# A fused layer kernel: the final shift laid into the output ahead, scaled rows added to it by accumulating transfers, and short low parts of the last group on GpSimd

## Chip, cores and metric

One core of a Trainium2 chip. The metric is the device time of one execution in microseconds (us); the kernel before was run three times, and one further execution was profiled.

## What is computed

One layer over 2048 positions of width 1024: a normalisation, a projection, convolutions and a gated delta rule, an output projection, a gated feed-forward block (1024 to 2 x 2816, then 2816 to 1024), and a last normalisation with its own scale and shift. Only the end matters here:

```python
        h = adaln(x, g_norm_ffn[layer], shift_f, scale_f)
        gt, up = jnp.split(h @ w_gate_up[layer], 2, axis=-1)
        x = x + gate_f[:, None, :] * ((jax.nn.silu(gt) * up) @ w_down[layer])
    shift_o, scale_o = jnp.split(c_act @ w_ada_final + b_ada_final, 2, axis=-1)
    return adaln(x, g_norm_final, shift_o, scale_o)
```

`adaln(x, g, shift, scale)` divides each row by its root mean square, multiplies by `g` and `1 + scale`, and adds `shift`, which is one row of 1024 numbers that is the same for all positions.

## The kernel before

All matrix products are made from split operands: a value is the sum of a rounded high part (`...h`, made by ScalarE) and a low part (`...l`, the difference, made by VectorE or GpSimd), and a product is three matmuls: high x high, high x low, low x high.

The last stage multiplies the hidden activations by `w_down`. The 2816 features are 22 blocks of 128, taken in pairs, and the pairs in six groups: group 0 has one pair, groups 1 to 5 two each. The outer loop runs over the groups, the inner one over eight slices `s`; a slice stands for two tiles of 128 positions, `(s, 0)` and `(s, 1)`. One (group, slice) is an item. Each tile has an accumulator `acc` (128 x 1024) in SBUF that lives through all groups.

In groups 1 to 5 an item's 2 x 2 block product is made with seven products in place of eight (Strassen's way): A11, S1, A12, S2, S4, S3 and A22, each of two pairs x three matmuls of 512 columns, so 42 matmuls per item. After each product, or second product into the same bank, VectorE adds the PSUM bank to half an accumulator (`add`, L1681, seven per item). S3 and A22 (`p7`, `p4`, the list `late`) are held back and run among the products of the next item. The order within an item is A11, S1, the last item's S3, A12, S2, S4, the last item's A22.

The item after next is loaded by `load_item` (L1542, two pieces `ra` of 448 KB, three buffers, on SyncE's queue). `split_item` (L1554 to 1573) splits the next item's pieces: `xh`, `xl` (5 of the 7 operands, 128 x 640) and `yh`, `yl` (the operands S3 and A22, 128 x 256). The high parts are ScalarE's (L1564). The low parts are subtractions at L1573, on the engine that `lo_engine` names: in groups 1 to 4 the first pair's are VectorE's and the second's GpSimd's; in the last group all are VectorE's.

The weights of the next group are prepared inside a group by `prep_group`: rows of `w_down` are loaded on SyncE's queue (L373), multiplied by a gate on GpSimd (L1610), then combined and split on VectorE and ScalarE. The last group has no such work.

In the last group a tile is finished as soon as its last addition is made, by `finish` (L1687), a generator that is advanced after every six matmuls: ScalarE squares and sums the row (L511), GpSimd makes the inverse root (L505, L506), VectorE scales the accumulator by it and by `go_d`, the gain (L1691), GpSimd adds the shift `so_d` (L1692), and SyncE's queue stores 512 KB (L1694). This is done for 15 tiles; the sixteenth, `(7, 1)`, goes through `finish_last` (L1697 to 1716), which splits the row in parts over the engines (GpSimd L1703, VectorE L1704, L1707, L1708, GpSimd's power L1709, then three pieces and two stores). The rows `go_d` and `so_d` lie in a DRAM row each (`final_d`) and are copied to all partitions once, in group 4 (L1663).

In this stage the order of instructions on an engine is that of a scheduler, not the order of the source: instructions of neighbouring steps may change places.

Of the kernel before, what the change touches and what calls it, by code (L numbers as in the profile page):

```python
# [15 lines left out]
ALU = mybir.AluOpType  # L16
# [4 lines left out]
P = 128  # L21
D = 1024
# [8 lines left out]
CH = BLK // P  # L31
# [169 lines left out]
def layer_kernel(ctx, tc, x, c, w_ada, b_ada, w_ada_final, b_ada_final, g_norm_mix, g_norm_ffn, g_norm_final,  # L201
                 w_in, conv_w_mix, conv_w_qkv, a_log, dt_bias, g_conv_out, g_dn_out, w_out, w_gate_up,
                 w_down, cst, out):
    nc = tc.nc
    x, out = x[0], out[0]
# [15 lines left out]
    def dense_ps():  # L221
        return pd.tile([P, 512], F32, name="pd")

    def misc_ps():
        return pm.tile([P, 512], F32, name="pm")
# [34 lines left out]
    def spawn(gen, delay=1):  # L260
        side.append([gen, delay, gen.__name__ not in FIRST_CHAINS])
        side.sort(key=lambda e: e[2])
# [245 lines left out]
    def sum_squares(t):  # L508
        ss = g0.tile([P, 1], F32, name="ss", bufs=4)
        junk = sp.tile([P, D], mybir.dt.bfloat16, name="ht", bufs=2)  # L510
        nc.scalar.activation(junk, t, AF.Square, accum_out=ss)  # L511
        rms_scale(ss, 1, D)
        return ss
# [149 lines left out]
    with ExitStack() as actx:  # L663
# [119 lines left out]
        for b in range(NB):  # L783
# [434 lines left out]
            for m in range(4):  # L1218
# [9 lines left out]
                u = ap_.tile([P, BLK + 3], F32, name="cb", bufs=2)  # L1228
# [17 lines left out]
            for n in range(2):  # L1246
# [27 lines left out]
                for t in range(CH):  # L1274
                    row = b * CH + t
# [12 lines left out]
    final_d = {n: dr.tile([1, D], F32, name=n) for n in ("go_d", "so_d")}  # L1288
# [89 lines left out]
    def work():  # L1378
        for q in (jobs, sums):
            while q:  # L1380
                try:
                    next(q[0])
                    break
                except StopIteration:
                    q.popleft()

    def work_off():
        while jobs or sums:
            work()
# [140 lines left out]
    last = len(groups) - 1  # L1530
# [3 lines left out]
    def load_item(n):  # L1534
        if n >= len(items):
            return
        g, s = items[n]
        raws[n] = []
        for i in groups[g]:
            w = 4 if i == 0 else 7  # L1540
            raw = dp.tile([P, 7, P], F32, name="ra", bufs=3)[:, :w, :]
            nc.sync.dma_start(raw, actd[s // CH, i][s % CH][:, :w, :])  # L1542
            raws[n].append(raw)
        if g == 0:
            for u in range(2):
                t = dp.tile([P, D], F32, name=f"acc{s}_{u}")
                nc.sync.dma_start(t, x1d[s // CH * 8 + u * CH + s % CH])
                accs[s, u] = t

    def lo_engine(g, q):  # L1550
        return nc.vector if q == 0 and g or g == last else nc.gpsimd


    def split_item(n):  # L1554
        if n >= len(items):
            return
        g, s = items[n]
        acts_d[n], todo = [], []
        for q, (i, raw) in enumerate(zip(groups[g], raws.pop(n))):
            X = {}  # L1560
            for e, c0, c1 in (("x", 0, 5 if i else 4),) + ((("y", 5, 7),) if i else ()):
                hl = [dp.tile([P, 5 if e == "x" else 2, P], F32R, name=e + p, bufs=4 if e == "x" else 6) for p in "hl"]
                hi, lo = (t[:, :c1 - c0, :] for t in hl)
                nc.scalar.copy(hi, raw[:, c0:c1, :])  # L1564
                todo.append((e, lo_engine(g, q), lo, raw[:, c0:c1, :], hi))
                for j in range(c0, c1):
                    X[(ORDER if i else FIRST)[j]] = [t[:, j - c0, :] for t in hl]
            acts_d[n].append(X)
        for e in "xy":
            yield  # L1570
            for f, eng, lo, raw, hi in todo:
                if f == e:
                    eng.tensor_sub(lo, raw, hi.bitcast(F32))  # L1573

    load_item(0)
    ahead = split_item(0)
    next(ahead)
    next(ahead, None)
# [70 lines left out]
    def prep_group(g):  # L1649
        if g <= last:  # L1650
            i, j = groups[g]
            DW[i], DW[j] = {}, {}
            yield from gate_pair(i)
            yield from down_weights(i, lambda: load_pair(j))
            yield
            yield from gate_pair(j)
            yield from down_weights(j, lambda: load_pair(groups[g + 1][0]) if g < last else None)
        if g == last:
            yield
            for n in ("go_d", "so_d", "g"):  # L1660
                fin[n] = wr.tile([P, D], F32, name="wraw")
                src = g_norm_final.rearrange("(o n) -> o n", o=1) if n == "g" else final_d[n]
                nc.sync.dma_start(fin[n], src.to_broadcast([P, D]))  # L1663
            yield
            yield
            yield
            nc.vector.scalar_tensor_tensor(fin["go_d"], fin["go_d"], 1.0, fin["g"], op0=ALU.add, op1=ALU.mult)

    fin = {}

    def dproduct(ps, parts, start):
        for q, (a, w) in enumerate(parts):
            (ah, al), (wh, wl) = a, w
            first = dict(start=start and q == 0, skip_group_check=not start)
            dmm(ps, ah, wh, stop=False, **first)
            first["start"] = False
            dmm(ps, ah, wl, stop=False, **first)
            dmm(ps, al, wh, stop=q == len(parts) - 1, **first)

    def add(s, u, ns, ps):  # L1680
        nc.vector.tensor_add(accs[s, u][:, ns], accs[s, u][:, ns], ps)  # L1681

    def row(s, u):
        r = s // CH * 8 + u * CH + s % CH
        return slice(r * P, (r + 1) * P)

    def finish(s, u):  # L1687
        t = accs[s, u]
        ss = sum_squares(t)
        yield 3  # L1690
        nc.vector.scalar_tensor_tensor(t, t, ss, fin["go_d"], op0=ALU.mult, op1=ALU.mult)  # L1691
        nc.gpsimd.tensor_add(t, t, fin["so_d"])  # L1692
        yield 2
        nc.sync.dma_start(out[row(s, u), :], t)  # L1694


    def finish_last(s, u):  # L1697
# [22 lines left out]
    for n, (g, s) in enumerate(items):  # L1720
        if s == 0:
            work_off()
            jobs.append(prep_group(g + 1))
        G, X = groups[g], acts_d.pop(n)
        ahead = split_item(n + 1)

        def parts(a, w):
            return [(x[a], DW[i][w]) for x, i in zip(X, G)]

        if g == 0:  # L1730
            for q in range(4):
                p = dense_ps()
                u, c0 = q // 2, q % 2
                r, cl = "A" + "12"[u], "12"[c0]
                dproduct(p, [(X[0][r + k], DW[0]["B" + k + cl]) for k in "12"], True)
                add(s, u, (h0, h1)[c0], p)
                if q == 0:
                    next(ahead, None)
                    load_item(n + 2)
                elif q == 1:  # L1740
                    for _ in ahead:
                        pass
                work()
            continue
        a, b, c_ = dense_ps(), misc_ps(), misc_ps()
        dproduct(a, parts("A11", "B11"), True)
        add(s, 0, h0, a)
        next(ahead, None)
        dproduct(c_, parts("S1", "T1"), True)
        add(s, 1, h1, c_)  # L1750
        work()
        if late:
            late[0]()
        next(ahead, None)
        dproduct(b, parts("A12", "B21"), True)
        add(s, 0, h0, b)
        work()
        dproduct(a, parts("S2", "T2"), False)
        add(s, 0, h1, a)
        next(ahead, None)  # L1760
        load_item(n + 2)
        dproduct(c_, parts("S4", "B22"), False)
        add(s, 0, h1, c_)
        work()
        if g == last:
            spawn(finish(s, 0), 1)
        if late:
            late[1]()
        work()

        def p7(a=a, s=s, q=parts("S3", "T3")):
            dproduct(a, q, False)
            add(s, 1, h1, a)

        def p4(a=a, s=s, q=parts("A22", "T4"), g=g):
            dproduct(a, q, False)
            add(s, 1, h0, a)
            if g == last and s < 2 * CH - 1:
                spawn(finish(s, 1), 1)

        late = p7, p4
# [27 lines left out]
```

## Time and profile before

| | |
|---|---|
| median of 3 runs | 2486.65 us (2485.29 to 2488.56) |
| the profiled execution, its own time | 2487.72 us |
| its span in the profile | 2485.9 us |
| busy, whole span: TensorE | 2356.5 us (95%) |
| VectorE | 1833.5 us (74%) |
| ScalarE | 1024.0 us (41%) |
| GpSimd | 644.7 us (26%) |
| mean rate of the transfers | 136 GB/s |

PE is TensorE, PEld its weight loads, DVE VectorE, ACT ScalarE, POOL GpSimd, SP SyncE (a q behind it: its queue). L1681 is line 1681 of the kernel. Times in the timeline are us from the start of the span. A busy share is an average over the whole program; a stretch of its own has its own limit, and the last group, some 90 us, is 4% of the span. The ends of matmuls are modelled and overlap: one lasts 0.39 us in the rows while they follow each other every 0.23 us.

### The profile page before, as it was taken

How to read it: one execution, taken by the hardware profiler on the slowest of the kernel's cores; microseconds unless marked ns; L12 is line 12 of the kernel's file. 1: busy time of each engine (PE TensorE's matmuls, PEld its weight loads, DVE VectorE, ACT ScalarE, POOL GpSimd, SP SyncE). 2: the span in 40 equal slices, each digit the busy share in tenths (PEclk: the TensorE clock that was granted, in tenths of full speed). 3: DMA queues.
4: the chain of work that ended last, by engine and by line, in shares of the span. 5: the costliest groups of instructions: out<-in, count | busy, mean ns of one | idle time of the engine just before them, and what ended most of it. 6: DMA issues, size and time to landing. Idle time of an engine off the chain costs nothing. (4 is left out here: it accounts for less than half of the span.)

```text
span 2485.9 us, 30764 instructions
## 1 busy us (share of the span) xinstructions
PE 2356.5 (95%) x11243; PEld 1937.9 (78%) x11243; DVE 1833.5 (74%) x2610; ACT 1024.0 (41%) x1771; POOL 644.7 (26%) x688
## 2 busy tenths in 40 slices
PE   5889999999899999998999999999999999999996
PEld 4778877888778877886878888878888877887774
DVE  6897759875897659788566566875665668888898
ACT  3633555344643464355543333533333323332232
POOL 2632255032722255212000000000000045444336
PEclk9999999999999999999999999999999999999999
DMA  7442446524452344236673333753433373333433
GB/s 244 119 106 68 145 140 174 156 90 155 138 149 78 118 148 111 69 115 199 193 234 108 92 115 101 245 169 94 119 101 99 106 269 131 119 120 106 137 126 115
DMA packets 397534, 336.98 MB, mean 136 GB/s; under 512 B 39475, under 2 KB 338748, under 8 KB 397382
## 3 DMA queue, kind: packets, MB, share of 16 engines
q1 hardware_dynamic: 397126, 334.91, 44.0%
q8 instruction: 88, 1.44, 0.2%
q14 instruction: 64, 0.52, 0.1%
q10 hardware_dynamic: 256, 0.10, 0.0%
HBM read 261.55 MB, written 73.41 MB: 135 GB/s over the span
## 5 line engine op out<-in xcount | busy, mean ns | idle before, releaser
L378 ACT CAST whi<-wraw 128x1024 fp32r<-128x1024 f32 x278 | 291.8, 1050 | 389.2 <-PE pd L311 191.4
L380 DVE TENSOR_TENSOR wlo<-wraw,whi 128x1024 fp32r<-128x1024 f32 x275 | 346.4, 1260 | 98.0 <-ACT whi L378 91.3
L311 PE MATMUL pd<-hTh,whi 128*128 128x512 f32 x896 | 369.7, 413 | 1.8 <-DVE hTh L540 1.6
L311 PE MATMUL pd<-hTl,whi 128*128 128x512 f32 x896 | 354.3, 395 | 1.8 <-DVE hTl L541 1.8
L311 PE MATMUL pd<-hTh,wlo 128*128 128x512 f32 x896 | 354.6, 396 | 1.5 <-DVE wlo L380 1.5
L1487 POOL TENSOR_TENSOR wraw<-wraw 128x1024 f32<-128x1024 f32 x2 | 5.0, 2504 | 780.3 <-DMA wraw<-in_w_down_dram 780.3
L311 PEld LDWEIGHTS pd<-hTh,wlo 128*128 128x128 f32 x896 | 170.7, 191 | 39.6 <-DVE wlo L380 2.4
L311 PEld LDWEIGHTS pd<-hTh,whi 128*128 128x128 f32 x896 | 171.9, 192 | 36.4 <-DVE hTh L540 3.1
L311 PEld LDWEIGHTS pd<-hTl,whi 128*128 128x128 f32 x896 | 171.8, 192 | 34.3 <-DVE hTl L541 2.6
L1441 DVE TENSOR_TENSOR sg<-sg,pd 128x512 f32<-128x512 f32 x44 | 30.2, 686 | 171.0 <-PE pd L311 171.0
L1681 DVE TENSOR_TENSOR acc<-acc,pd 128x512 f32<-128x512 f32 x192 | 127.9, 678 | 29.2 <-PE pd L311 29.0
L1564 ACT CAST xh<-ra 128x640 fp32r<-128x640 f32 (+1 forms) x88 | 62.6, 719 | 199.6 <-PE pm L311 160.1
L1176 DVE SCALAR_TENSOR_TENSOR cv<-cb,pcb,cv 128x512 f32<-128x512 f32 x144 | 136.4, 947 | 3.7
L1573 POOL TENSOR_TENSOR xl<-ra,xh 128x640 fp32r<-128x640 f32 (+1 forms) x40 | 65.7, 1644 | 160.8 <-ACT xh L1564 156.5
L1281 POOL TENSOR_TENSOR cv<-cv 128x512 f32<-128x512 f32 x32 | 45.6, 1435 | 207.8 <-DVE cv L1280 123.7
L1681 DVE TENSOR_TENSOR acc<-acc,pm 128x512 f32<-128x512 f32 x120 | 81.5, 679 | 17.2 <-PE pm L311 16.8
L311 PE MATMUL pd<-whi,ym 128*128 128x512 f32 x256 | 86.5, 398 | 0.0
L1610 POOL TENSOR_TENSOR wraw<-wraw 128x512 f32<-128x512 f32 x40 | 70.4, 1783 | 43.0 <-DMA wraw<-in_w_down_dram 35.0
L311 PE MATMUL pd<-S2h,whi 128*128 128x512 f32 x176 | 69.4, 394 | 4.7 <-ACT whi L378 4.7
L311 PE MATMUL pd<-A22h,whi 128*128 128x512 f32 x176 | 69.1, 392 | 4.6 <-DVE sg L1441 4.6
L311 PE MATMUL pm<-S4h,whi 128*128 128x512 f32 x176 | 69.2, 393 | 2.7 <-ACT sg L1435 2.7
L311 PE MATMUL pd<-S2h,wlo 128*128 128x512 f32 x176 | 69.6, 395 | 0.5 <-DVE wlo L380 0.5
(456 smaller groups left out, 6333.7 us busy)
## 6 DMA issues: line engine op xcount, KB each, us to landing
wraw<-in_w_in_dram SPq DMA_DIRECT2D x112, 512.0 KB, 4.0
wraw<-in_w_gate_up_dram SPq DMA_DIRECT2D x88, 512.0 KB, 4.2
ra<-act SPq DMA_DIRECT2D x80, 448.0 KB, 4.0
act<-S SPq DMA_DIRECT2D x80, 256.0 KB, 2.5
act<-act SPq DMA_DIRECT2D x68, 256.0 KB, 2.2
wraw<-in_w_ada_dram SPq DMA_DIRECT2D x32, 512.0 KB, 3.8
wraw<-in_w_out_dram SPq DMA_DIRECT2D x32, 512.0 KB, 3.6
wraw<-in_w_down_dram SPq DMA_DIRECT2D x22, 512.0 KB, 3.5
```

Source lines behind the costliest of these rows:

```text
L311: mm(*args, **kw)
L378: nc.scalar.copy(hi, raw)
L380: (lo_engines.popleft() if lo_engines else nc.vector).tensor_sub(lo, raw, hi.bitcast(F32))
L1176: nc.vector.scalar_tensor_tensor(cv, cb[:, t:t + BLK], tap[t], cv, op0=ALU.mult, op1=ALU.add)
L1281: nc.gpsimd.tensor_add(xr, xr, yo)
L1441: nc.vector.tensor_add(s5[i], s5[i], a[i])
L1487: nc.gpsimd.tensor_mul(r, r, first_w["gate"])
L1564: nc.scalar.copy(hi, raw[:, c0:c1, :])
L1573: eng.tensor_sub(lo, raw, hi.bitcast(F32))
L1610: nc.gpsimd.tensor_mul(r[:, hs], r[:, hs], gate_f[:, hs])
L1681: nc.vector.tensor_add(accs[s, u][:, ns], accs[s, u][:, ns], ps)
```

## The change

`lo_engine` is given the operand's letter too. In the last group it now names VectorE for `x` and GpSimd for `y`, for both pairs; in the groups before nothing changes.

`lay_shift` is new: in group 2, at the start of each item, SyncE's queue copies the shift row from DRAM to the 128 output rows of each of the slice's tiles (DRAM to DRAM, 512 KB each), except for tile `(7, 1)`: 15 transfers.

`finish` no longer adds the shift on GpSimd and no longer stores from SyncE's queue. Behind L1691, GpSimd issues one transfer that adds the scaled accumulator to what lies in the output rows. `finish_last` is as before.

```diff
-    def lo_engine(g, q):
-        return nc.vector if q == 0 and g or g == last else nc.gpsimd
+    def lo_engine(g, q, e):
+        return nc.vector if (e == "x" if g == last else q == 0 and g) else nc.gpsimd
...
-                todo.append((e, lo_engine(g, q), lo, raw[:, c0:c1, :], hi))
+                todo.append((e, lo_engine(g, q, e), lo, raw[:, c0:c1, :], hi))
...
+    def lay_shift(s):
+        for u in range(2):
+            if (s, u) != (2 * CH - 1, 1):
+                nc.sync.dma_start(out[row(s, u), :], final_d["so_d"].to_broadcast([P, D]))
+
     def finish(s, u):
         t = accs[s, u]
         ss = sum_squares(t)
         yield 3
         nc.vector.scalar_tensor_tensor(t, t, ss, fin["go_d"], op0=ALU.mult, op1=ALU.mult)
-        nc.gpsimd.tensor_add(t, t, fin["so_d"])
-        yield 2
-        nc.sync.dma_start(out[row(s, u), :], t)
+        nc.gpsimd.dma_start(out[row(s, u), :], t, accum_op=ALU.add)
...
+        if g == 2:
+            lay_shift(s)
```

## Rows read from the trace of the kernel before

**Rows 1.** The page's first line.

```profile
span 2485.9 us, 30764 instructions
```

**Rows 2.** Busy time by stretches: the busiest transfers, two items of group 2, one of the last.

```profile
core 0: us, PE busy (x) PEld busy (x) DVE busy (x) ACT busy (x) POOL busy (x), PEclk, DMA share, GB/s
2035.00:2045.00 10.00, 10.00 (x46) 8.28 (x45) 8.11 (x13) 3.58 (x5) 4.91 (x5) 1.00 0.96 388
...
2185.00:2194.56 9.56, 9.56 (x44) 7.92 (x43) 6.60 (x11) 2.21 (x5) 2.45 (x3) 1.00 0.29 98
2194.56:2204.08 9.52, 9.52 (x44) 7.88 (x43) 6.56 (x11) 2.17 (x5) 2.45 (x3) 1.00 0.30 96
...
2412.26:2424.74 12.48, 10.47 (x44) 7.65 (x42) 12.36 (x14) 4.51 (x8) 7.25 (x7) 1.00 0.45 157
```

**Rows 3.** Waits, 2390 to 2486 us: us in total, times, longest (TensorE's, SyncE's queue).

```profile
PE pd L311 <- DVE acc L1681: 11.0, 10, 2.3
PE pm L311 <- DVE acc L1681: 3.8, 5, 2.4
...
SPq L1694 <- POOL acc L1692: 70.5, 15, 8.6
```

**Rows 4.** Groups by form, VectorE, three items (2412.26 to 2449.72 us): busy us, mean ns.

```profile
L1691 DVE SCALAR_TENSOR_TENSOR acc<-acc,ss,wraw 128x1024 f32<-128x1024 f32 x7 | 14.2, 2028 | 0.5
L1681 DVE TENSOR_TENSOR acc<-acc,pd 128x512 f32<-128x512 f32 x12 | 8.1, 675 | 0.0
L1573 DVE TENSOR_TENSOR yl<-ra,yh 128x256 fp32r<-128x256 f32 x6 | 7.9, 1322 | 0.0
L1573 DVE TENSOR_TENSOR xl<-ra,xh 128x640 fp32r<-128x640 f32 x6 | 4.9, 811 | 0.0
```

**Rows 5.** Timeline inside one item of the last group: start us, us, instruction.

```profile
2411.05 1.28 DVE L1691 SCALAR_TENSOR_TENSOR acc<-acc,ss,wraw 128x1024 f32<-128x1024 f32 x1
...
2412.99 2.40 POOL L1692 TENSOR_TENSOR acc<-acc,wraw 128x1024 f32<-128x1024 f32 x1
2413.45 3.02 DVE L1691 SCALAR_TENSOR_TENSOR acc<-acc,ss,wraw 128x1024 f32<-128x1024 f32 x1
...
2416.55 2.39 POOL L1692 TENSOR_TENSOR acc<-acc,wraw 128x1024 f32<-128x1024 f32 x1 [1.17 <-DVE acc L1691]
2416.99 2.23 DVE L1573 TENSOR_TENSOR yl<-ra,yh 128x256 fp32r<-128x256 f32 x1
...
2422.41 0.41 DVE L1573 TENSOR_TENSOR yl<-ra,yh 128x256 fp32r<-128x256 f32 x1
```

**Rows 6.** Timeline of TensorE: its first stalled matmul of the last group, and its last matmul.

```profile
2410.99 0.50 PE L311 MATMUL pd<-whi,xh 128*128 128x512 f32 x1 [0.58 <-DVE acc L1681]
...
2474.26 0.40 PE L311 MATMUL pd<-vh,yl 128*128 128x512 f32 x1
```

**Rows 7.** Timeline of the end: last addition, the blocked one-column instruction, the power.

```profile
2476.44 0.67 DVE L1681 TENSOR_TENSOR acc<-acc,pd 128x512 f32<-128x512 f32 x1
...
2477.54 2.78 POOL L1692 TENSOR_TENSOR acc<-acc,wraw 128x1024 f32<-128x1024 f32 x1
2478.05 2.29 DVE L1708 SCALAR_TENSOR_TENSOR ss<-ss 128x1 f32<-128x1 f32 x1
...
2480.42 0.55 POOL L1709 TENSOR_TENSOR ss<-ss,mhalf 128x1 f32<-128x1 f32 x1
```

**Rows 8.** Transfers: issues with KB and us to landing; a store's issue in the timeline.

```profile
ra<-act SPq DMA_DIRECT2D x80, 448.0 KB, 4.0
...
out_dram<-acc SPq DMA_DIRECT2D x15, 512.0 KB, 2.9
...
2480.35 0.33 SPq L1694 DMA_DIRECT2D out_dram<-acc  x1
```

**Rows 9.** Waits for transfers in group 2 (2140 to 2230 us): us in total, times, longest.

```profile
POOL wraw L1610 <- DMA wraw<-in_w_down_dram: 14.0, 2, 7.3
...
ACT xh L1564 <- DMA ra<-act: 4.6, 3, 2.5
```

**Rows 10.** Timeline of GpSimd in group 2: a short low part.

```profile
2186.57 0.92 POOL L1573 TENSOR_TENSOR yl<-ra,yh 128x256 fp32r<-128x256 f32 x1
```

## The prediction

> **What bounds the kernel now.** I read the page first for the span, then the busy time by stretches, then the waits of the last stretch, then the groups by form and the order of time inside one item. Only the last group of feature blocks (eight items, from about 2387 us) differs from the groups before it: there VectorE is full and TensorE is not. In group 2 an item takes 9.56 us with TensorE busy for all of it; in the last group the same 42 matmuls take 12.48 us, TensorE is busy for 10.47 and VectorE for 12.36 [rows 2]. The waits agree: TensorE waits for the additions of L1681, 11.0 and 3.8 us, and for nothing else [rows 3]. So the pace of the last group is VectorE's queue.
>
> What fills that queue is not arithmetic alone. The same scaling of L1691 takes 1.28 us when GpSimd is quiet and 3.02 us when GpSimd's addition of the shift (L1692, 2.40 us) runs; the short low part `yl` takes 0.41 us alone and 2.23 us beside the next L1692 [rows 5]. Over three periods the seven L1691 average 2028 ns, the six `yl` 1322 ns [rows 4]: each item loses two long blocks to GpSimd's additions.
>
> **VectorE's load after.** The change takes both `yl` and both L1692 out of VectorE's way: `yl` moves to GpSimd, L1692 disappears. What is left per item, by durations: seven additions x 0.675 = 4.73, two `xl` x 0.811 = 1.62, two L1691 x 1.28 = 2.56 [rows 4, 5]; 8.9 us, and a little less, since neighbours overlap by about 0.07 us. That is below TensorE's 42 x 0.2267 = 9.52 us, 0.2267 being group 2's pace (an item's 42 matmuls in 9.52 us, and once in 9.56 [rows 2]). TensorE becomes the bound again.
>
> **What that gives.** TensorE's first stall is the 0.58 us before 2410.99; before it TensorE runs through, since its PSUM banks let it get ahead. So nothing is won before 2410.41. From there to the last matmul's end (2474.26 + 0.40 = 2474.66) [rows 6] are 33 products: S2, S4 and the late A22 of item 3, seven in each of items 4 to 7, and the last two; 33 x 6 = 198 matmuls x 0.2267 = 44.9, plus 0.17 for the last one's drain, gives an end at 2455.5. Gain **19.2 us** (the 14.8 us of waits, and some 0.27 us at each of 15 restarts).
>
> **The tail.** Now 2485.9 - 2474.66 = 11.2 us [rows 1, 6]. Call the end of the matmuls E. The last addition starts 1.8 us after E, because a blocked L1691 stands ahead of it, and then the one-column L1708 takes 2.29 us behind the last L1692 [rows 7]. After the change: the L1691 of item 6's second half still stands ahead in VectorE's order. Its matmuls end 12 x 0.2267 = 2.7 us before E; addition, square, power take it to about E + 0.2, L1691 to E + 1.5, the last addition to E + 2.2. From there T 0.98, L1708 about 0.1, power 0.55 and gaps make 1.75 us, and from the power's end (2480.97) to the end of the span 4.9 us as now. E + 8.9. Gain **2.3 us** (3.8 if the scheduler puts the addition first).
>
> **The accumulating transfers.** No row shows one; GpSimd issues no transfer at all before. Three prices.
> Issue on GpSimd: from 0.33 us (SyncE's issue of the same store [rows 8]) to 2.40 us (the addition it replaces). I take 1.2, between them: GpSimd's work, but on descriptors and not on 1024 columns. GpSimd then has per item its present 7.25 less 2 x 2.40 [rows 2, 5], so 2.45, plus two `yl` x 0.92 [rows 10], plus 2.4: 6.7 of 9.5 us. No bound; at 2.4 each it would be 9.1. Behind an issue that waits for L1691 stand the next `yl` and the row sums. The `yl` is used only by S3 and A22, which run one item late, so 2 us don't show; its lateness would be seen in the `ra` loads, whose buffers it frees. Those gain in turn: SyncE no longer holds stores that waited 70.5 us for L1692 [rows 3], with loads queued behind.
> Landing: from 2.9 us (plain store) to 4.0 + 2.9 = 6.9 us (a 448 KB load, then the store [rows 8]). I take 5: one more read than a store, overlapped in part. The last one is issued at E + 1.5, out at E + 2.7, landed at E + 7.7, before the plain store of the last row at E + 8.9: hidden. At the upper ends (2.4 and 6.9) it lands at E + 10.8, 1.9 us too late.
> Occupancy T of all 16 engines: from 1.35 us (512 KB at the 388 GB/s of the busiest stretch [rows 2]) to 6.9. I take 2.7, two reads at that rate. The first is ready at 2389 and the eight `ra` pieces loaded after that need some 16 us (2 each, between 1.2 at 388 GB/s and the 4.0 of their landing), so the 15 done by 2464 allow (2464 - 2389 - 16) / 15 = 3.9 us each. Hidden.
> The Trainium skill, Collectives: The Full Stack, The bandwidth ceiling, says that a reducing transfer is slower for its two source reads and not for its addition, at about half a copy's rate; by it T would be an estimated 2.6 us, and the sum unchanged. No row here shows it.
>
> **The shift laid ahead.** Fifteen 512 KB transfers, issued from SyncE in group 2, two per item (0.33 us each of SyncE). No gain is possible there, TensorE is busy 9.56 of 9.56 [rows 2]. They share the engines with `ra` and `w_down` loads: 1 MB at 388 GB/s is 2.7 us per item. ScalarE already waits 4.6 us for `ra` there and GpSimd 14.0 us, twice, for `w_down` [rows 9], with TensorE full all the same. At worst both weight waits grow by 2.7 us and hold GpSimd's `xl` behind them: 5.4. I take 0.5, near zero, since these waits are off the path.
>
> **Residue.** GpSimd's `yl` reads SBUF too and can block an `xl` or L1691; at L1573's present cost on GpSimd, 0.92 us x 2, VectorE has 0.6 us of room at least. I take 0.3 us per item lost, 1.5 in all.
>
> Sum: 19.2 + 2.3 - 0.5 - 1.5 = 19.5 us. The profiled execution took 2487.72 us, 1.8 more than its span and 1.07 more than the median, 2486.65. 2487.72 - 19.5 = 2468.2; in terms of the median **2467 us**.
>
> **Rivals.**
> Forecast, chance 0.57: 2462 to 2472 by the bounds above.
> VectorE stays the bound (0.16). For it: blocking took up to 2.2 us per event [rows 5], and two `yl` x 0.92 on top of 8.9 is 10.75 us per item. Against: `yl` is now 256 columns, not 1024, and often falls beside an addition from PSUM, which is never slowed (0.675 throughout [rows 4]). Price: (10.75 - 9.52) x 4.7 items = 5.8 in place of 1.5: 2471; with waits for row sums, up to 2476. The Trainium skill, SBUF — State Buffer, Who interferes with whom, says that a VectorE instruction with two SBUF inputs contends with a GpSimd instruction that reads SBUF and the second fully blocks; that speaks for this rival, and the trace agrees (2.23 beside 0.41 us).
> The other side: transfers pile up (0.16, of it 0.11 slower). Place: the DMA engines from 2389 on. From T = 3.9 the last sum lands after the rest; at (2485.9 - 2389 - 16 - 2) / 15 = 5.3 all is given back; at 6.9 the end is 2389 + 16 + 103 + 2 = 2510, 2511 us in terms of the median. For it: no row has a read-modify-write. Against: rates of 388 GB/s.
> GpSimd held while its transfer runs (0.06), so that the change does not free it: 2.45 + 1.84 + 2 x 4 = 12.3 us per item, the present pace; only the tail is won: 2484.
> The laid rows delay group 2 (0.05): + 5: 2472.
>
> **Numbers.** A measurement of this kernel tells 0.2%, 5 us, from no change. Faster by more: 0.57 + 0.16 + 0.05 + 0.01 + 0.05 = 0.84. Within: 0.04, mostly the held GpSimd. Slower: 0.12. The range 2462 to 2478 holds the forecast, the blocked VectorE and the delayed group 2; it leaves out piled-up transfers and the held GpSimd.
>
> **What would show it.** After: items of the last group 9.5 to 9.8 us apart with TensorE's waits for L1681 nearly gone; L1691 near 1.3 us; no `yl` on VectorE; the last matmul near 2456 and the end 9 us later, set by the plain store of the last row. Wrong: L1691 or `xl` over 2 us beside GpSimd's `yl`; accumulating rows landing ever later after issue; GpSimd's issues taking several us; the span's end released by an accumulating transfer; gaps on TensorE between 2148 and 2225.

## The result, and the profile after

| | before | after |
|---|---|---|
| median us (lowest to highest, runs) | 2486.65 (2484.36 to 2489.83, 5) | 2472.88 (2470.6 to 2476.78, 5) |
| ratio, 95% interval | | 0.9942 [0.9932, 0.9953] |
| the profiled execution, own time; span | 2487.72; 2485.9 | 2476.78; 2475.0 |

The change makes the kernel 13.8 us faster. The forecast was 19.7: inside the range, and 5.9 us too hopeful. The profiled execution after is the slowest of its five, so its span shows only 10.9 us of gain.

**The last group does what was forecast, up to its last product.** Busy time by stretches in the kernel after, one item of the last group (columns as in [rows 2]), and TensorE's waits from 2376 us to the end:

```profile
2420.00:2429.50 9.50, 9.50 (x44) 7.87 (x43) 8.69 (x12) 4.38 (x8) 6.00 (x9) 1.00 0.93 209
```
```profile
PE pd L311 <- DVE acc L1681: 2.2, 1, 2.2
```

Against [rows 2] and [rows 3]: an item takes 9.50 us and not 12.48, TensorE is full, VectorE has 0.8 us of room, and one wait of 2.2 us is left of fifteen that made 14.8. The DMA share, 0.93, stands close under 1. The groups by form of the kernel after, 2376 to 2476 us (busy us, mean ns, idle before), answer to [rows 4] and [rows 10]; L1697 is now the scaling (L1691 before), L1698 the accumulating transfer:

```profile
L1697 DVE SCALAR_TENSOR_TENSOR acc<-acc,ss,wraw 128x1024 f32<-128x1024 f32 x15 | 19.3, 1285 | 4.7 <-POOL ss L506 3.9
...
L1573 POOL TENSOR_TENSOR yl<-ra,yh 128x256 fp32r<-128x256 f32 x15 | 16.9, 1144 | 25.5 <-ACT yh L1564 17.8 <-PE pd L311 7.7
...
L1573 DVE TENSOR_TENSOR xl<-ra,xh 128x640 fp32r<-128x640 f32 x15 | 14.5, 965 | 2.5 <-ACT xh L1564 2.5
L1698 POOL DMA_DIRECT2D out_dram<-acc x15 | 13.5, 903 | 6.6 <-DVE acc L1697 6.5
```

No scaling is blocked any more: 1285 ns in the mean, where it was 2028.

**The accumulating transfers fit.** The transfers of the same stretch of the kernel after: GpSimd's queue (packets, MB, share of 16 engines), then issues with KB and us to landing:

```profile
q0 software_dynamic: 2160, 7.87, 48.1%
...
out_dram<-acc POOLq DMA_DIRECT2D x15, 512.0 KB, 5.7
...
DMA to landing us min/median/max: 5.4/5.7/7.7
```

48.1% of 100 us over 15 transfers is T = 3.2 us of all 16 engines each. The landings (the last line: all 15) lie between 5.4 and 7.7 us and do not grow: the first three have a median of 5.6, the last four of 5.8.

**The loss is at the other end of the stage.** The laying (L1691 in the kernel after) was written into group 2, from about 2140 us on. The timeline of SyncE's queue in the kernel after shows it elsewhere:

```profile
1991.88 0.71 SPq L474 DMA_DIRECT2D so_d<-ht  x2
...
1994.14 1.86 SPq L1691 DMA_DIRECT2D out_dram<-so_d  x3
...
1999.26 5.08 SPq L1691 DMA_DIRECT2D out_dram<-so_d  x5
2009.90 0.38 SPq L1355 DMA_DIRECT2D act<-act  x1
2010.38 1.16 SPq L1542 DMA_DIRECT2D ra<-act  x1
```

L474 writes the shift row. From then on nothing holds the laying, and the scheduler issued eight of the fifteen one after the other, ahead of the first load `ra` of the last stage (the other seven between 2069.9 and 2094.4, around the start of group 1). What that did is in the timelines of ScalarE and TensorE, first after, then before (there with the issue of the load):

```profile
2022.12 0.62 ACT L1564 CAST xh<-ra 128x512 fp32r<-128x512 f32 x1 [11.47 <-DMA ra<-act]
...
2022.79 0.79 PE L311 MATMUL pd<-whi,xh 128*128 128x512 f32 x1 [12.78 <-ACT xh L1564]
```
```profile
2008.49 0.46 SPq L1542 DMA_DIRECT2D ra<-act  x1
...
2011.34 0.62 ACT L1564 CAST xh<-ra 128x512 fp32r<-128x512 f32 x1 [1.44 <-DMA ra<-act]
...
2012.01 0.50 PE L311 MATMUL pd<-whi,xh 128*128 128x512 f32 x1 [2.75 <-ACT xh L1564]
```

The load is issued 1.9 us later than before (2010.38, 2008.49), but what waits for it starts 10.8 us later: most of the delay lies behind its issue, with the engines full. TensorE's first matmul of the stage waits 12.78 us where it waited 2.75. The stretches around it (TensorE busy and its matmuls, granted clock, DMA share, GB/s), before and then after:

```profile
2002.00:2022.00 20.00, 16.61 (x66) 0.91 0.67 209
2022.00:2042.00 20.00, 19.57 (x85) 1.00 1.02 399
2042.00:2062.00 20.00, 20.00 (x90) 1.00 0.52 181
2062.00:2082.00 20.00, 18.15 (x73) 0.91 0.51 180
```
```profile
2002.00:2022.00 20.00, 8.02 (x36) 0.80 1.02 262
2022.00:2042.00 20.00, 19.08 (x73) 0.86 0.99 353
2042.00:2062.00 20.00, 20.00 (x90) 1.00 0.81 312
2062.00:2082.00 20.00, 18.15 (x79) 1.00 0.57 189
```

By 2062 us the kernel after has run 199 matmuls, the one before 241: 42 fewer, 9.5 us at 0.2267. Six come back in the next 20 us, where the kernel before runs partly at the lower clock (0.91) and the one after does not.

**A measure for what follows.** The stage starts at another time in each execution (2003 to 2012 us), for reasons ahead of all edits here. So I also count from t0, the start of that first wait: before, 2012.01 - 2.75 = 2009.26, leaving 476.6 us to the end of the span; after, 2022.79 - 12.78 = 2010.01, leaving 465.0. This measure comes from one profiled execution each. The changed kernel, profiled twice, gives 465.0 and 462.4 (8 below), so single differences under some 3 us tell nothing.

### The profile page after: what moved, and what is told of

Read it like the earlier page. It is cut to its first block, busy times and chain, and to the rows that moved or that the text cites. A ratio compares the mean times of both kernels' runs of the same rounds, so it can differ in the third digit from the quotient of the medians.

```text
span 2475.0 us, 30786 instructions
## 1 busy us (share of the span) xinstructions
PE 2356.1 (95%) x11243; PEld 1942.8 (78%) x11243; DVE 1806.3 (73%) x2594; ACT 1024.4 (41%) x1771; POOL 638.8 (26%) x704
## 4 chain that ended last, share of the span: by engine, by line
PE 50%; DVE 6%; DMA 3%; ACT 2%; issue 2%; POOL 2%; SPq 0%; DVEq 0%; ACTq 0%; POOLq 0%
PE pd L311 30%; PE pm L311 18%; DVE acc L1681 1%; DMA y<-xT 1%; DMA ra<-act 1%; DVE wlo L380 1%; DVE cv L1176 0%; DVE dl L1602 0%; DMA wraw<-in_w_gate_up_dram 0%; DMA y<-in_w_ada_final_dram 0%; ACT whi L378 0%; DVE xl L1573 0%; POOL wraw L1610 0%; DMA A12d<-y 0%; PE pm L565 0%
## 5 line engine op out<-in xcount | busy, mean ns | idle before, releaser
L1681 DVE TENSOR_TENSOR acc<-acc,pd 128x512 f32<-128x512 f32 x192 | 127.7, 679 | 41.9 <-PE pd L311 41.1
L1681 DVE TENSOR_TENSOR acc<-acc,pm 128x512 f32<-128x512 f32 x120 | 81.7, 681 | 18.0 <-PE pm L311 17.6
```

## The experiments

My theory after the result: the forecast is right for the last group, and the laying, by its place in SyncE's queue, costs the difference. The rival: the laying's delay is hidden, and the loss lies in the last group (accumulation, or GpSimd's `yl`). Kernels 1 to 4 ran on one chip, 5 to 8 on another, 9 and 10 on a third, each time beside the kernel before.

| kernel | median us (runs) | before, same chip | ratio, 95% interval | t0 to end, us |
|---|---|---|---|---|
| 1 laying alone | 2495.26 (10) | 2488.65 | 1.0026 [1.0015, 1.0038] | 482.9 |
| 2 no laying | 2468.34 (4) | 2488.65 | 0.9918 [0.9891, 0.9944] | 454.9 |
| 3 laying pinned in group 2 | 2471.1 (4) | 2488.65 | 0.9933 [0.9909, 0.9957] | 456.8 |
| 4 `yl` back on VectorE | 2475.69 (8) | 2488.65 | 0.9958 [0.9942, 0.9975] | 462.4 |
| 5 spread, pinned, order edge | 2467.94 (6) | 2486.05 | 0.9928 [0.9911, 0.9945] | 458.1 |
| 6 plain stores, no laying | 2458.81 (1) | 2486.05 | none | 451.9 |
| 7 `yl` move alone | 2479.63 (10) | 2486.05 | 0.9973 [0.9960, 0.9985] | 469.7 |
| 8 the changed kernel again | 2473.85 (6) | 2486.05 | 0.9947 [0.9931, 0.9964] | 462.4 |
| 9 spread, pinned | 2466.07 (5) | 2486.61 | 0.9916 [0.9900, 0.9932] | 455.1 |
| 10 as 9, `yl` on VectorE | 2468.95 (6) | 2486.61 | 0.9926 [0.9909, 0.9943] | 454.6 |

**1. The laying alone**, in the kernel before.

```diff
+        if g == 2:
+            lay_shift(s)
```

> The kernel before, with the fifteen laying transfers added as in the change and nothing else (the stores overwrite the laid rows later). The scheduler puts them at the same places of SyncE's queue as in the changed kernel: eight of them ahead of the first loads of the last stage. Theory (the early laying is what the change pays): TensorE waits some 10 to 13 us for the first piece ra, where it waited 2.7, and the time is 2494 to 2499 us, 8 to 12 above before. Rival (the laying is hidden, what is missing from the gain was lost in the last group): 2485 to 2489 us, and the first wait as before.

TensorE's timeline in kernel 1:

```profile
2022.94 0.80 PE L311 MATMUL pd<-whi,xh 128*128 128x512 f32 x1 [12.52 <-ACT xh L1564]
```

The wait comes with the laying and nothing else of the change. The time is 6.6 us longer (3.7 to 9.5 by the interval), less than the 8 to 12 expected and than the 9.8 by which the wait grew. TensorE's other waits of the stage make 21.8 us where they made 25.3 before, so part is taken back.

**2. No laying.** The changed kernel without the calls; 15 of 16 tiles lack their shift.

```diff
-        if g == 2:
-            lay_shift(s)
```

> The changed kernel without the laying transfers: the accumulating ones stay, so the shift is missing from 15 of the 16 tiles. Theory (early laying costs 9 to 10 us): 2461 to 2466 us, last group as in the changed kernel, first wait near 2.7 us. Rival (lost in the last group): 2471 to 2474 us.

From t0 it ends 476.6 - 454.9 = 21.7 us earlier than before; the forecast's terms without the laying and the residue were 19.2 + 2.3 = 21.5. The medians give 20.3. The time, 2468.34, lies above the 2461 to 2466 expected and below the rival's range; its four executions spread over 11.8 us. The first wait is 3.34 us.

**3. The laying pinned.** The same transfers, forbidden to leave their place in the source.

```diff
-                nc.sync.dma_start(out[row(s, u), :], final_d["so_d"].to_broadcast([P, D]))
+                tc.keep_in_program_order(nc.sync.dma_start(out[row(s, u), :], final_d["so_d"].to_broadcast([P, D])))
```

> The changed kernel with each laying transfer kept, on SyncE's queue, behind what stands before it in the source, so that they are issued in group 2, two per item. Theory (the place costs, not the bytes): TensorE full in group 2, 2461 to 2467 us. Second theory (the bytes cost wherever they go: 1 MB more per item delays the loads ra and w_down there): gaps of TensorE in group 2, 2470 to 2475 us. Rival (lost in the last group): 2471 to 2474 us with no gaps in group 2.

All transfers of the laying in kernel 3 (duration of the issue in ns, first and last start, then landing), and then SyncE's transfers from 2120 to 2220 us, in kernel 3 and in kernel 2 (packets, MB, share of 16 engines):

```profile
L1691 SPq DMA_DIRECT2D out_dram<-so_d x15: 496/588/754, 2131.1 to 2213.8; - x15
...
DMA to landing us min/median/max: 4.4/5.7/7.1
```
```profile
q1 hardware_dynamic: 5745, 19.63, 60.3%
```
```profile
q1 hardware_dynamic: 3600, 11.80, 35.6%
```

Now they stand where the prediction thought they stood. TensorE's first wait is 3.56 us. In and just behind group 2 it waits 1.7 and 2.4 us, about where kernel 2, without laying, waits 1.2 and, in three waits, 2.7, so these are not new with the laying. From t0 the end is 456.8, beside 454.9 in kernel 2: a difference too small to tell from nothing. The time does not settle it: 2471.1 lies in the range expected if the bytes cost wherever they go, and the interval overlaps that of the changed kernel. What decides for the place is the first wait, and kernel 9. In the changed kernel the same 15 landed in 6.1 to 14.9 us.

**4. `yl` back on VectorE**, in the changed kernel.

```diff
-        return nc.vector if (e == "x" if g == last else q == 0 and g) else nc.gpsimd
+        return nc.vector if q == 0 and g or g == last else nc.gpsimd
```

> The changed kernel with the short low parts of the last group on VectorE again. Theory (GpSimd's additions were what blocked VectorE; without them a yl costs 0.41 us): VectorE has 8.9 + 0.8 = 9.7 us of work per item by durations, some less by overlap, against TensorE's 9.52; items 9.5 to 9.8 us apart, 2472 to 2475 us, at most 2 above the changed kernel. Rival (each yl moved saved its 2.2 or 0.4 us, so that this part of the change carries about half of the gain): items over 11 us apart, 2479 to 2483 us.

One item of the last group in kernel 4, same columns as above:

```profile
2420.00:2429.50 9.50, 9.50 (x44) 7.86 (x43) 8.87 (x14) 4.36 (x9) 4.17 (x6) 1.00 0.94 208
```

TensorE stays full: with L1692 gone nothing blocks `yl` on VectorE (0.42 us each), and 8.87 us fit in 9.5. The interval overlaps that of the change, and from t0 the kernel ends as the changed one does in 8 (462.4). Beside the removal of the addition, the move of `yl` is worth nothing that can be measured here.

**5. Spread, pinned, with an order edge.** One laid tile per item over groups 2 and 3, and L1697 of tile (7, 0) behind the last item's S3 addition, for which the last product's bank waited 2.17 us.

```diff
+        if g in (2, 3):
+            lay_shift(s, g - 2)
...
+        with tc.issue_after(fin["p7"]) if s == 2 * CH - 1 else ExitStack():
             nc.vector.scalar_tensor_tensor(t, t, ss, fin["go_d"], op0=ALU.mult, op1=ALU.mult)
```

> The changed kernel with the laying transfers kept in their place on SyncE's queue and spread, one per item over groups 2 and 3, and with one order edge at the end: the scaling L1697 of tile (7, 0) stands behind the addition that the last product's PSUM bank waits for. Theory (place and burst of the laying are its cost; the last stall of 2.2 us is VectorE's order): first wait near 3 us, no new gaps in groups 2 and 3, the last product's wait gone; 9 to 13 us below the changed kernel on the same chip. Rival (an accumulating transfer sets the end once the rest is shorter): the last one lands after the plain store and the gain is 2 to 4 us less.

The end of kernel 5 (L1709 GpSimd's half addition of `finish_last`, L1699 the scaling, L1681 the last addition, L1722 the stores):

```profile
2452.10 0.50 PE L311 MATMUL pd<-whi,yh 128*128 128x512 f32 x1 [0.78 <-DVE acc L1681]
...
2453.90 1.25 POOL L1709 TENSOR_TENSOR acc<-acc,wraw 128x512 f32<-128x512 f32 x1
...
2453.96 2.27 DVE L1699 SCALAR_TENSOR_TENSOR acc<-acc,ss,wraw 128x1024 f32<-128x1024 f32 x1 [0.65 <-POOL ss L506]
...
2456.16 0.68 DVE L1681 TENSOR_TENSOR acc<-acc,pd 128x512 f32<-128x512 f32 x1
...
2459.30 1.25 SPq L1722 DMA_DIRECT2D out_dram<-acc  x2
```

A miss: 5.9 us below kernel 8, not the 9 to 13 expected. The bank's wait shrank to 0.78 us, but the matmuls end at 2453.8 and the last addition starts only at 2456.16, behind a scaling that now takes 2.27 us beside GpSimd's L1709. The wait was moved, not removed, and the final stores land 7.1 us after their issue instead of some 4.6 (after: 2475.0 - 2470.36), beside two late accumulating transfers; that is the rival's sign. Kernel 9, without the edge, ends 3.0 us earlier from t0.

**6. Plain stores**, from GpSimd, without laying and without accumulation: 15 tiles without their shift, one run.

```diff
-        nc.gpsimd.dma_start(out[row(s, u), :], t, accum_op=ALU.add)
+        nc.gpsimd.dma_start(out[row(s, u), :], t)
```

> The changed kernel without laying, and with GpSimd's transfers as plain stores: the shift is missing from 15 tiles. It prices the accumulation by itself. Theory (two reads instead of one): landing near 4 us in place of 5.7, occupancy of the 16 engines about 1.6 us in place of 3.2 per transfer, the issue on GpSimd 0.9 us as before. Rival (the cost is that of GpSimd's way of issuing, not of the addition): landing and occupancy as with the addition.

The transfers of kernel 6 (issue in ns, then landing) and its queue between 2376 and 2457 us:

```profile
L1698 POOL DMA_DIRECT2D out_dram<-acc x15: 531/606/807, 2382.9 to 2450.4; - x15
...
DMA to landing us min/median/max: 2.8/2.9/3.4
```
```profile
q0 software_dynamic: 2160, 7.87, 23.7%
```

23.7% of 81 us over 15 is T = 1.3 us. So accumulating takes 3.2 / 1.3 = 2.5 times the engines, twice the landing (5.7 beside 2.9) and 0.3 us more of GpSimd per issue. All three prices of the plain store are below those expected (1.6, about 4, and an issue of 0.9 where 0.61 came), so more of the cost is the accumulation's than I thought. The end, 451.9 from t0, is 3.0 us earlier than kernel 2's; one run can't say how much of that is accumulation.

**7. The `yl` move alone**, in the kernel before.

```diff
-        return nc.vector if q == 0 and g or g == last else nc.gpsimd
+        return nc.vector if (e == "x" if g == last else q == 0 and g) else nc.gpsimd
```

> The kernel before with only the short low parts of the last group moved to GpSimd. Theory (the block is GpSimd's addition, and without yl only one of the two additions still falls beside an operation of VectorE with two SBUF inputs): VectorE 10.0 to 10.5 us per item in place of 12.48, TensorE 9.52, so 4.7 items x 2.0 to 2.5 = 9 to 12 us below before. Rival (the block moves on to the next such operation, xl): items over 11.5 us apart, at most 5 us below before.

VectorE and GpSimd inside one item of kernel 7 (L1692 still the shift's addition):

```profile
2424.06 2.40 POOL L1692 TENSOR_TENSOR acc<-acc,wraw 128x1024 f32<-128x1024 f32 x1
2424.13 3.42 DVE L1691 SCALAR_TENSOR_TENSOR acc<-acc,ss,wraw 128x1024 f32<-128x1024 f32 x1
...
2427.62 2.39 POOL L1692 TENSOR_TENSOR acc<-acc,wraw 128x1024 f32<-128x1024 f32 x1 [1.16 <-DVE acc L1691]
...
2429.26 1.44 DVE L1573 TENSOR_TENSOR xl<-ra,xh 128x640 fp32r<-128x640 f32 x1
```

Alone the move brings 6.4 us (items 11.45 us apart, not 12.48). The result lies between the two expectations: `yl`'s own time leaves VectorE, but a part of the block passes on to the second scaling and to `xl`.

**8. The changed kernel again**, on the chip of 5 to 7, unedited.

> The changed kernel once more, on the chip of these runs, to compare with. Both theories: its ratio to before as first measured, 0.993 to 0.996, and the first wait of the last stage 11 to 13 us.

The first wait is there again, 13.34 us. The kernel ends 14.2 us earlier than before from t0, and 12.2 by the medians.

**9. Spread and pinned**, without the edge of 5.

```diff
-        if g == 2:
-            lay_shift(s)
+        if g in (2, 3):
+            lay_shift(s, g - 2)
```

> The changed kernel with the laying transfers kept in place and spread, one per item over groups 2 and 3, without the order edge at the end. Theory (the edge only moved the wait of the end from TensorE to VectorE, and half the burst per item halves what the laying costs in group 2): from the start of the first wait of the last stage to the end of the span 454.5 to 456.5 us, where the changed kernel took 462.4 and 465.0, the pinned one 456.8 and the one without laying 454.9; a ratio to before of 0.990 to 0.994. Rival (the edge helped, something else in that run cost time): 458 us or more.

TensorE's waits of kernel 9 from 2000 us to the end:

```profile
PE pd L311 <- DVE acc L1681: 10.3, 6, 2.2
PE pd L311 <- ACT xh L1564: 3.4, 1, 3.4
```

The best version: 20.5 us faster than before, some 7 us more than the change gained. From t0 it ends at 455.1, as if nothing were laid (kernel 2: 454.9). Spread thin over stretches that used 0.3 of the engines [rows 2], the laying has no cost that can be measured. TensorE ends 446.6 us after t0, 18.8 earlier than before's 2474.66 - 2009.26 = 465.4, and the tail gains 2.8; the forecast had 19.2 and 2.3.

**10. As 9, with `yl` on VectorE** (the edit of 4).

> The same with the short low parts on VectorE again, so only the accumulating half of the change. Theory (with GpSimd's additions gone VectorE has room for them: 8.9 us busy in 9.5 with them, 8.7 without): within 1.5 us of the run with them on GpSimd, from the first wait to the end and in time. Rival (with the early wait gone, VectorE is short of room again): TensorE waits for L1681 in every item and the end is 3 us or more later.

The same as kernel 9 within what can be told (454.6 and 455.1 from t0; the medians are 2.9 us apart, more than the 1.5 expected, but the intervals overlap). It agrees with 4, with the laying out of the way.

## Why the prediction was right, and where it was off

**What bounds, and what that gives: right.** With VectorE's blocks gone TensorE sets the pace, at 9.50 us per item. Kernels 2 and 9 show the two terms without the laying's delay: 21.7 and 21.6 us from t0, for 21.5 forecast.

That the sum comes out so closely is in part luck. In the last group of kernel 9 TensorE still loses an estimated 3.0 us: 2.2 in the last product's wait, 0.27 at its restart, and some 0.6 in the matmuls behind it, which ran at the lower clock. Before, it lost 14.8 and fifteen restarts of 0.27, which is 18.9 (the prediction names these two parts for its 19.2). So the last group saves an estimated 15.8 us and the tail 2.8, together 18.6. The other 3.0 lie ahead of the last group, where no edit of kernel 9 saves time; there the two profiles of the changed kernel also differ by 3.0 us (from t0 to the start of the 56th addition L1681 from the end: 379.4 and 376.4). No run shows these 3 us to be the change's.

**VectorE's load: right.** 8.69 us busy for "8.9 us, and a little less"; the scaling 1285 ns for 1.28.

**The tail: right in sum, not in its order.** TensorE does stall once more: the last product's bank waits 2.17 us for an addition that stands behind a scaling. So the matmuls end later against VectorE's queue and the last addition starts at once. The end of the kernel after (last matmul, last addition, power, final stores):

```profile
2464.40 0.63 PE L311 MATMUL pd<-whi,yh 128*128 128x512 f32 x1 [2.17 <-DVE acc L1681]
...
2466.53 0.63 PE L311 MATMUL pd<-vh,yl 128*128 128x512 f32 x1
...
2467.20 0.69 DVE L1681 TENSOR_TENSOR acc<-acc,pd 128x512 f32<-128x512 f32 x1 [1.38 <-PE pd L311]
...
2468.99 0.56 POOL L1713 TENSOR_TENSOR ss<-ss,mhalf 128x1 f32<-128x1 f32 x1 [1.28 <-DVE ss L1712]
...
2470.36 1.25 SPq L1720 DMA_DIRECT2D out_dram<-acc  x2
```

With the matmuls' end E at 2467.16 the span ends at E + 7.8, forecast E + 8.9, and now 11.2.

**The accumulating transfers: right that they hide, sizes within the bounds.** Issue 0.90 us (1.2 taken), landing 5.7 (5), T 3.2 (2.7). The limit worked out was T = 3.9; a DMA share of 0.93 in an item says how near it is. So the rivals of piled-up transfers and of a held GpSimd fall: the landings do not grow, and GpSimd is busy for 6.00 us of an item. The Trainium skill, Collectives: The Full Stack, The bandwidth ceiling, puts the reducing transfers of a ReduceScatter at about half a copy's rate. That agrees in direction; kernel 6 measures 2.5 times, and the measurement decides.

**Residue: the block is seen, but not the 1.5 us.** `xl` grows from 811 to 965 ns beside GpSimd's `yl` (in kernel 4, with `yl` on VectorE, it takes 820), 0.3 us an item, and VectorE's 0.8 us of room absorbs it. The Trainium skill, SBUF — State Buffer, Who interferes with whom, says which pairs block; kernel 7 shows such blocks (3.42 us for a scaling beside L1692, where 1.28 is the time alone). They cost time only where the blocked engine has no room.

**The step that failed: the laying's term.** The prediction's words were "Fifteen 512 KB transfers, issued from SyncE in group 2, two per item" and "I take 0.5, near zero, since these waits are off the path." The rows it rested on, [rows 2] and [rows 9], are from group 2, and there the estimate is fair: pinned there or spread over two groups, the laying shows no cost beyond the 3 us that single profiles leave open. But nothing ties it to group 2. It was issued some 120 to 140 us ahead of kernel 3's places, eight of the fifteen in the one stretch where TensorE has nothing to do until a load lands. The price: 6.6 us timed alone (kernel 1), 6.5 to 8.3 by the medians of the changed kernel, in both its measurements, against 2 and 9, and 7.5 to 10 by the profiles from t0. The rival "the laid rows delay group 2" had the sign and a size (5 us), not the place. The section on the kernel before says that the scheduler may exchange instructions; the prediction never asked what held the new ones back.

The size was low too, but only for tiles that stand in one burst: "1 MB at 388 GB/s is 2.7 us per item", 1.35 us a tile. Busy time by stretches in the kernel before and the kernel after, while the laying had the engines nearly to itself (columns as in [rows 2]):

```profile
1994.00:2004.00 10.00, 10.00 (x46) 8.29 (x45) 2.06 (x3) 2.77 (x4) 7.47 (x6) 1.00 0.22 82
2004.00:2010.00 6.00, 5.26 (x24) 4.02 (x22) 2.67 (x5) 0.60 (x1) 0.13 (x1) 1.00 0.20 53
```
```profile
1994.00:2004.00 10.00, 10.00 (x46) 8.29 (x45) 2.15 (x2) 3.10 (x5) 5.82 (x4) 1.00 0.92 217
2004.00:2010.00 6.00, 6.00 (x27) 4.66 (x25) 3.32 (x4) 0.00 (x0) 1.97 (x2) 1.00 1.02 254
```

The engines are full at 217 to 254 GB/s. The extra bytes, (217 - 82) x 10 + (254 - 53) x 6 = 2556 KB in 16 us, are 4.9 tiles of 524 KB: an estimated 3.3 us a tile beside the other transfers. Eight of them, begun at 1994, fill some 26 us, to about 2020; the first `ra` landed at 2022. Of the engines' own time the extra share, (0.92 - 0.22) x 10 + (1.02 - 0.20) x 6 = 11.9 us, makes an estimated 2.4 us a tile. Pinned, a tile took less: (60.3% - 35.6%) of 100 us over 15, in kernels 3 and 2, is 1.6 us, near the 1.35. Why it takes more in the burst no run here shows.

**What stays open.** Whether the last product's 2.17 us can be won; kernel 5 only moved it. And why the part of the program ahead of the last stage differs by up to 9 us between executions; t0 removes it from the comparisons and does not explain it. Inside the stage some 3 us between executions remain, as said above.

## What to carry to other kernels

A transfer without a dependence has no place in time: before it is priced by the stretch it was written into, ask what holds it back, look at the queue for the earliest point at which it could start, and pin it or spread it where the engines are idle. Where one block has two ends, either half of a change may relieve it: here the move of `yl` was worth 6 us alone and nothing measurable beside the other half, so the halves are priced each with and without the other. An addition that blocks a full engine can go into the store's transfer, as long as 2.5 times the store's engine time still fits under the pace of the stage.

## What the runs showed of the hardware

Accumulating into DRAM from GpSimd's queue: 3.2 us of 16 engines per 512 KB, beside 1.3 for the plain store, and still with rates of 209 GB/s at a share of 0.93.

Copying one row to 128 rows inside DRAM, eight times in one burst, filled the engines at 217 to 254 GB/s, an estimated 2.4 us of 16 engines per 512 KB. Pinned two per item among loads, it took 1.6 us.

The granted clock after an idle stretch: behind the 12.8 us of waiting the mean was 0.86 over the next 20 us, with matmuls at half pace, the 1.2 GHz level, at first (0.50 from 2022.8 to 2026). Behind the 2.17 us wait near the end the last six matmuls of the kernel after ran at half pace (a granted clock of 0.54, 0.63 us in the rows, 0.43 us apart, about 1.2 us lost), but in kernels 3 and 10, behind the same 2.17 us, they took 0.39 to 0.40 after a first one of 0.50. What decides between the two no run here shows.
